# ga2 spread over 32 rows of the gate and up projections, with six places for its K-tiles

## The chip, the cores and the metric

The kernel runs on one NeuronCore of a Trainium2 chip. The metric is the device time of one execution in microseconds (us), as the median of several runs. The engines are TensorE (PE; its weight loads stand apart as PEld), VectorE (DVE), ScalarE (ACT), GpSimd (POOL) and SyncE (SP), whose queue issues nearly all loads here.

## What is computed

One layer of a diffusion backbone: a modulated RMS norm, an input projection to three parallel groups of heads (a recurrent scan, a short convolution, a Fourier mix), an output projection with a gated residual, then a modulated RMS norm, a SwiGLU FFN and a second gated residual. The six modulation vectors, 2048 long each, come from one product:

```python
m = jax.nn.silu(cvec) @ w + b
sh1, sc1, ga1, sh2, sc2, ga2 = jnp.split(m[:, None, :], 6, axis=-1)
...
x = x + ga1 * yx
x = x + ga2 * ffn(modulate(rms_norm(x, norm_ffn), sh2, sc2), w_gate, w_up, w_down)
```

The change concerns ga2 alone. It is not needed until the down projection's results are added to x. Token count is 256, D is 2048 and the FFN is 5632 wide.

## The kernel before

All numbers are float32. The large products keep full precision by splitting both sides into a high and a low part (the high part in a reduced matmul format), with three matmuls for one: high x high, high weight x low input, low weight x high input (`mm3`, line 249).

The FFN (`phase_ffn`, line 1101) has a gate/up part of 44 **rows** f, each giving 128 of the 5632 hidden columns, and a down part of 16 tiles. A row takes 4 **blocks** of weights: gate and up, each in two halves of 8 K-tiles. `wblock` (line 271) loads a block of 512 KB on SyncE's queue (w), ScalarE casts it to the high part (whi, line 266), and VectorE or, for every third block, POOL forms the low part (wlo, line 269). w, whi and wlo have three places each. TensorE then runs 24 matmuls for the block, so 96 for a row. At a row's end ScalarE takes silu of the gate half, VectorE multiplies it with the up half (line 1167, called vi in the code), and the product is split into HH (ScalarE) and HL (VectorE, line 269). Rows 0 and 1 are run together, while the normalised input XH and XL is formed.

w_mod's last four groups are formed on VectorE as a sum over K-tiles of a 128 x 512 piece of the matrix times one number per partition; 16 K-tiles make 512 of the 2048 x 4 columns, and 16 such vectors i = 0 to 15 make all four groups. Vectors 0 to 11 are formed earlier in the kernel. Vectors 12 to 15 are ga2 and are formed in the FFN by `modvec` (line 1081). Each K-tile is one load of 256 KB on SyncE's queue (line 1088) into one of two places of the buffer `ar`, and one multiply (line 1090, the first) or multiply-add (line 1092) on VectorE, into one of two accumulators. `modvec_end` (line 1094) sums over the partitions by four matmuls of a column of ones (line 233, out st), and adds the bias (line 1077).

`ar` lies in the memory of an earlier tile, so that the profile calls both the K-tiles and the accumulators XH; XH<-wmb is a K-tile's load. The profile's XH in gu<-XH is the normalised input, another tile of that name.

A scheduler orders each engine's instructions from the program text and its own estimate of times, after which each engine works through its list in order. `issue_after(vi.ins)` makes the VectorE instructions of the block under it stand behind row f's product in VectorE's list. The loads have no such tie and stand where the scheduler puts them. SyncE works through one list as well: a load that waits for its place holds all loads behind it.

Of the kernel before, what the change touches and what calls it, by code (L numbers as in the profile page):

```python
# [19 lines left out]
KT = D // P  # L20
# [180 lines left out]
class Builder:  # L201
# [876 lines left out]
                                     pm[:, :2 * npc].rearrange("p (j s) -> p j s", s=2)[:, :, s],  # L1078
                                     bm[:, 2 + g, o:o + npc], op=ALU.add)

    def modvec(self, i):

        nc, T = self.nc, self.t
        v2 = lambda ap: ap.rearrange("p (a t) -> p a t", t=L)
        acc = self.ar[:, 2 * (i % 2):2 * (i % 2) + 2]
        for k in range(KT):
            w = self.ar[:, 4 + 2 * (k % 2):6 + 2 * (k % 2)]
            nc.sync.dma_start(w, v2(self.a["wmb"][i, k]))
            if k == 0:
                nc.vector.tensor_scalar_mul(acc, w, self.sc[:, k, 1:2])  # L1090
            else:
                nc.vector.scalar_tensor_tensor(acc, w, self.sc[:, k, 1:2], acc, op0=ALU.mult, op1=ALU.add)  # L1092
# [8 lines left out]
    def phase_ffn(self, st):  # L1101
        tc, nc, a = self.tc, self.nc, self.a
        V, S, G, T = nc.vector, nc.scalar, nc.gpsimd, self.t
        fp = st.enter_context(tc.tile_pool(name="fp", bufs=2, reuse_waits="tile"))
        wsf = st.enter_context(tc.tile_pool(name="wsf", bufs=3, reuse_waits="tile"))
        fps = st.enter_context(tc.tile_pool(name="fps", bufs=2, space=PSUM, reuse_waits="tile"))
        X1 = self.X1
        XH = T(self.cp, [P, KT, L], F32R, "XH1")
        XL = T(self.cp, [P, KT, L], F32R, "XL1")
        self.modps, self.modtag = fps, "st"  # L1110

        T(fp, [P, 48], F32, "gap", 1)
        HH = T(fp, [P, NFF, L], F32R, "HH", 1)
        HL = T(fp, [P, NFF, L], F32R, "HL", 1)


        uh = self.uh
        ul = HL[:, NFF - 17:].rearrange("p f t -> p (f t)")[:, :KT * (L + 2)].rearrange("p (k t) -> p k t", k=KT)
        V.tensor_tensor(ul[:, :, L:], self.mod[:, 1].unsqueeze(2).to_broadcast([P, KT, 2]),
                        uh[:, :, L:].bitcast(F32), op=ALU.subtract)  # L1120
        for k in range(KT):
            V.scalar_tensor_tensor(ul[:, k, :L], X1[:, k], self.mod[:, 2, k:k + 1], uh[:, k, :L].bitcast(F32),  # L1122
                                   op0=ALU.mult, op1=ALU.subtract)
        self.heng = lambda n: nc.scalar
        self.cnt = 0
        self.leng = lambda n: nc.gpsimd if n <= 10 or n % 3 == 0 else nc.vector
        def gate_up(fs, xh, xl, norm=None):

            pgu = [T(fps, [P, 2 * L], F32, f"gu{w}")[:, :xh.shape[2]] for _ in fs for w in range(2)]
            for g in range(0, KT, G8):  # L1130
                for i, f in enumerate(fs):
                    for w in range(2):
                        with tc.issue_after(self.lasts):
                            h, lo = self.wblock(a["wgu"][f, w, :, g:g + G8], G8, G8, wsf)
                        for j in range(G8):
                            k = g + j
                            self.mm3(pgu[2 * i + w], h[:, j], lo[:, j], xh[:, k], xl[:, k], k == 0, k == KT - 1)
                        if norm is not None and (g, i, w) == (0, 0, 1):
                            S.copy(norm, self.rms_finish(self.x1s, fp, fps, L, "st", True))
            return pgu  # L1140

        for f in range(NFF):
            if f == 0:
                rs = T(fp, [P, L], F32, "rs", 1)
                pgs = gate_up((0, 1), uh, ul, rs)
                for k in range(KT):
                    xn = T(fp, [P, L], F32, "xn")
                    bias = self.mod[:, 1, k:k + 1]
                    V.scalar_tensor_tensor(xn, X1[:, k], self.mod[:, 2, k:k + 1], rs, op0=ALU.mult, op1=ALU.mult)  # L1149
                    S.activation(XH[:, k], xn, AF.Identity, bias=bias)  # L1150
                    V.scalar_tensor_tensor(XL[:, k], xn, bias, XH[:, k].bitcast(F32), op0=ALU.add, op1=ALU.subtract)  # L1151
                self.ar = self.wide(F32)[:, :, :L]
            sg = T(fp, [P, L], F32, "sg")
            if f < 2:
                pg, pu = pgs[2 * f:2 * f + 2]
                b = T(fp, [P, 2], F32, "b")
                V.tensor_copy(b[:, 0:1], pg[:, L:L + 1])
                V.tensor_copy(b[:, 1:2], pu[:, L:L + 1])
                V.tensor_tensor(sg, pg[:, :L], rs, op=ALU.mult)
                S.activation(sg, sg, AF.Silu, bias=b[:, 0:1])  # L1160
                su = T(fp, [P, L], F32, "xn")
                V.tensor_tensor(su, pu[:, :L], rs, op=ALU.mult)
                vi = V.scalar_tensor_tensor(sg, su, b[:, 1:2], sg, op0=ALU.add, op1=ALU.mult)
            else:
                pgu = gate_up((f,), XH, XL)
                S.activation(sg, pgu[0], AF.Silu)
                vi = V.tensor_tensor(sg, sg, pgu[1], op=ALU.mult)
            self.split(HH[:, f], HL[:, f], sg, S, V)
            if f % 8 == 3 and f < 32:
                with tc.issue_after(vi.ins):  # L1170
                    self.modvec(12 + f // 8)
            if f % 8 == 7 and f < 32:
                self.modvec_end(12 + f // 8)
        S.activation(self.x1s[:, :1], self.ones32[:, :1], AF.Sqrt)
        pst = T(fps, [P, L], F32, "st")
        for m in range(KT):
            pd = T(fps, [P, L], F32, "dn")
            for f0 in range(0, NFF, G8):
                nf = min(G8, NFF - f0)
                h, lo = self.wblock(a["wdn"][m, :, f0:f0 + nf], nf, G8, wsf)  # L1180
                for j in range(nf):
                    f = f0 + j
                    self.mm3(pd, h[:, j], lo[:, j], HH[:, f], HL[:, f], f == 0, f == NFF - 1)
            V.scalar_tensor_tensor(X1[:, m], pd, self.mod[:, 3, m:m + 1], X1[:, m], op0=ALU.mult, op1=ALU.add)
            sq = T(fp, [P, L], F32, "sq")
            S.square(sq, X1[:, m])
            self.rms_add(pst, sq, m)
            V.tensor_scalar_mul(X1[:, m], X1[:, m], self.vec("norm_final", m))
        rstd = self.rms_finish(pst, fp, fps, L, "st")
        rs = T(fp, [P, L], F32, "xn")  # L1190
        S.copy(rs, rstd)
        for k in range(0, KT, 2):
            o = self.ar[:, k:k + 2]
            for j in range(2):
                (G if k % 6 == 4 else V).tensor_tensor(o[:, j], X1[:, k + j], rs if k % 6 == 4 else rstd, op=ALU.mult)
            (nc.sync if k % 4 else nc.scalar).dma_start(self.out[:, k:k + 2], o)
# [16 lines left out]
```

## Time and profile before

| what | us |
|---|---|
| median of 3 runs | 1873.53 |
| lowest, highest | 1870.32, 1878.7 |
| the profiled execution | 1890.59 |
| its span, first to last instruction | 1888.8 |
| TensorE busy in it | 1733.7 |
| VectorE, ScalarE, POOL busy | 1107.4, 830.1, 802.8 |

The gate/up rows lie between 1080 and 1617 us of the span, the down tiles from 1617 to its end. The page has the busy shares; the chain of waits follows the work back from the last instruction, at each step to what released it, so its pieces add up to the span; a wait row names the engine that waited, what for, the total in us, the number of times and the longest one.

### The profile page before, as it was taken

How to read it: one execution, taken by the hardware profiler on the slowest of the kernel's cores; microseconds unless marked ns; L12 is line 12 of the kernel's file. 1: busy time of each engine (PE TensorE's matmuls, PEld its weight loads, DVE VectorE, ACT ScalarE, POOL GpSimd, SP SyncE). 2: the span in 40 equal slices, each digit the busy share in tenths (PEclk: the TensorE clock that was granted, in tenths of full speed). 3: DMA queues.
4: the chain of work that ended last, by engine and by line, in shares of the span. 5: the costliest groups of instructions: out<-in, count | busy, mean ns of one | idle time of the engine just before them, and what ended most of it. 6: DMA issues, size and time to landing. Idle time of an engine off the chain costs nothing.

```text
span 1888.8 us, 44826 instructions
## 1 busy us (share of the span) xinstructions
PE 1733.7 (92%) x18552; PEld 1587.2 (84%) x18552; DVE 1107.4 (59%) x1883; ACT 830.1 (44%) x1657; POOL 802.8 (43%) x718
## 2 busy tenths in 40 slices
PE   7888999999898899899898889999999999999997
PEld 4667898888787787687776688999999999999996
DVE  4445347787888777768784696454545434333223
ACT  2213355566655555444452443434344444433332
POOL 1223455467666665555661442322222232233332
PEclk9999999999999999999997989999999999999998
DMA  9884224355455443454441247676767666565554
GB/s 343 293 273 136 77 72 142 118 159 165 142 172 157 129 147 105 143 152 118 138 132 42 88 145 224 212 239 210 223 206 233 208 185 189 178 181 183 178 181 133
DMA packets 139229, 318.75 MB, mean 169 GB/s; under 512 B 14225, under 2 KB 40465, under 8 KB 139025
## 3 DMA queue, kind: packets, MB, share of 16 engines
q1 hardware_dynamic: 137936, 314.84, 53.1%
q8 instruction: 145, 2.38, 0.5%
q10 hardware_dynamic: 1088, 1.05, 0.2%
q14 instruction: 60, 0.48, 0.1%
HBM read 313.74 MB, written 2.10 MB: 167 GB/s over the span
## 4 chain that ended last, share of the span: by engine, by line
PE 40%; DVE 8%; DMA 6%; ACT 1%; issue 1%; POOL 0%; DVEq 0%; SPq 0%; ACTq 0%
PE gu L233 18%; PE dn L233 13%; DMA XH<-wmb 6%; PE pj L233 3%; PE acc L233 2%; PE st L233 1%; PE iv L233 1%; DVE XH L1092 1%; DVE macc L1063 1%; DVE XL L1151 1%; PE pp L233 1%; DVE HL L1122 0%; DVE xn L1149 0%; DVE XL L997 0%; DVE eb L729 0%
## 5 line engine op out<-in xcount | busy, mean ns | idle before, releaser
L269 POOL TENSOR_TENSOR wlo<-w,whi 128x512 fp32r<-128x512 f32 (+2 forms) x309 | 518.9, 1682 | 746.2 <-ACT whi L266 701.8
L266 ACT CAST whi<-w 128x1024 fp32r<-128x1024 f32 (+2 forms) x472 | 400.5, 849 | 565.7 <-PE gu L233 182.9
L233 PE MATMUL gu<-XH,wlo 128*128 128x256 f32 (+1 forms) x1408 | 398.5, 283 | 16.6 <-DVE wlo L269 14.9
L233 PE MATMUL gu<-XH,whi 128*128 128x256 f32 (+1 forms) x1408 | 397.8, 283 | 4.6 <-ACT whi L266 4.0
L269 DVE TENSOR_TENSOR wlo<-w,whi 128x1024 fp32r<-128x1024 f32 (+1 forms) x175 | 205.7, 1176 | 304.4 <-ACT whi L266 303.7
L233 PE MATMUL gu<-XL,whi 128*128 128x256 f32 x1344 | 376.6, 280 | 0.1
L233 PE MATMUL pj<-XH,whi 128*128 128x256 f32 x1016 | 285.6, 309 | 5.6 <-DVE XL L997 3.2
L233 PEld LDWEIGHTS gu<-XH,wlo 128*128 128x128 f32 x1408 | 269.0, 191 | 19.5 <-DVE wlo L269 17.2
L233 PEld LDWEIGHTS gu<-XH,whi 128*128 128x128 f32 x1408 | 271.3, 193 | 6.0 <-ACT whi L266 5.3
L233 PE MATMUL pj<-XL,whi 128*128 128x256 f32 x1016 | 257.6, 282 | 0.6 <-DVE XL L269 0.6
L233 PE MATMUL pj<-XH,wlo 128*128 128x256 f32 x1016 | 257.3, 282 | 0.0
L233 PEld LDWEIGHTS gu<-XL,whi 128*128 128x128 f32 x1344 | 255.2, 190 | 0.3 <-DVE XL L1151 0.3
L233 PE MATMUL dn<-HL,whi 128*128 128x256 f32 x704 | 199.4, 283 | 0.0
L233 PE MATMUL dn<-HH,whi 128*128 128x256 f32 x704 | 197.8, 281 | 0.0
L233 PE MATMUL dn<-HH,wlo 128*128 128x256 f32 x704 | 197.8, 281 | 0.0
L233 PEld LDWEIGHTS pj<-XH,whi 128*128 128x128 f32 x1016 | 181.8, 191 | 16.7 <-ACT whi L266 3.1
L233 PEld LDWEIGHTS pj<-XL,whi 128*128 128x128 f32 x1016 | 182.0, 191 | 2.4 <-issue 0.9
L233 PEld LDWEIGHTS pj<-XH,wlo 128*128 128x128 f32 x1016 | 181.0, 191 | 2.6 <-POOL whi L268 1.7
L1063 DVE SCALAR_TENSOR_TENSOR macc<-wm,sc,macc 128x512 f32<-128x512 f32 x180 | 170.1, 945 | 0.9
L233 PEld LDWEIGHTS dn<-HH,whi 128*128 128x128 f32 x704 | 135.1, 192 | 0.0
L233 PEld LDWEIGHTS dn<-HL,whi 128*128 128x128 f32 x704 | 132.1, 188 | 1.4
L233 PEld LDWEIGHTS dn<-HH,wlo 128*128 128x128 f32 x704 | 132.2, 188 | 0.0
(306 smaller groups left out, 2837.3 us busy)
## 6 DMA issues: line engine op xcount, KB each, us to landing
w<-wgu SPq DMA_DIRECT2D x176, 512.0 KB, 4.6
wm<-wmb SPq DMA_DIRECT2D x192, 256.0 KB, 3.1
w<-wdn SPq DMA_DIRECT2D x80, 512.0 KB, 4.3
w<-wib SPq DMA_DIRECT2D x148, 256.0 KB, 3.2
wm<-wma SPq DMA_DIRECT2D x64, 512.0 KB, 6.9
XH<-wmb SPq DMA_DIRECT2D x64, 256.0 KB, 4.1
w<-wout SPq DMA_DIRECT2D x48, 256.0 KB, 3.3
wa<-wia SPq DMA_DIRECT2D x16, 416.0 KB, 8.0
```

The lines of the kernel that those rows point to most:

```text
L233: self.last = self.nc.tensor.matmul(out, lhsT=lhsT, rhs=rhs, start=start, stop=stop)
L266: he.copy(hi, src)
L269: le.tensor_tensor(lo, src, hi.bitcast(F32), op=ALU.subtract)
L1063: V.scalar_tensor_tensor(acc, w, self.sc[:, k, 1:2], acc, op0=ALU.mult, op1=ALU.add)
L1092: nc.vector.scalar_tensor_tensor(acc, w, self.sc[:, k, 1:2], acc, op0=ALU.mult, op1=ALU.add)
L1151: V.scalar_tensor_tensor(XL[:, k], xn, bias, XH[:, k].bitcast(F32), op0=ALU.add, op1=ALU.subtract)
```

## The change

Two K-tiles of ga2 stand in each of the rows 0 to 31, instead of 16 in each of the rows 3, 11, 19 and 27. They use six places of `ar` by the K-tile's number, instead of two. A vector's column matmuls and its bias stand in the text after row 8, 16, 24 and 32, instead of 7, 15, 23 and 31.

```diff
-    def modvec(self, i):
+    def modvec(self, i, ks):
...
-        for k in range(KT):
-            w = self.ar[:, 4 + 2 * (k % 2):6 + 2 * (k % 2)]
+        for k in ks:
+            w = self.ar[:, 4 + 2 * (k % 6):6 + 2 * (k % 6)]
             nc.sync.dma_start(w, v2(self.a["wmb"][i, k]))
...
-            if f % 8 == 3 and f < 32:
+
+            if f < 32:
                 with tc.issue_after(vi.ins):
-                    self.modvec(12 + f // 8)
-            if f % 8 == 7 and f < 32:
-                self.modvec_end(12 + f // 8)
+                    self.modvec(12 + f // 8, (2 * (f % 8), 2 * (f % 8) + 1))
+            if f % 8 == 0 and 0 < f <= 32:
+                self.modvec_end(11 + f // 8)
```

SyncE's list before, at the second burst (row 11's text). w_ numbers are weight blocks in the order of the rows, XH<-wmb is a K-tile of ga2:

```order
L276 DMA w_2854_17681<-wgu 128x1024
L276 DMA w_2860_17718<-wgu 128x1024
L1088 DMA XH_2684_16225<-wmb 128x2x256 x2
L276 DMA w_2863_17748<-wgu 128x1024
L1088 DMA XH_2684_16225<-wmb 128x2x256
L276 DMA w_2866_17778<-wgu 128x1024
L1088 DMA XH_2684_16225<-wmb 128x2x256
L276 DMA w_2869_17808<-wgu 128x1024
L1088 DMA XH_2684_16225<-wmb 128x2x256 x2
L276 DMA w_2875_17845<-wgu 128x1024
```

The same place of SyncE's list now. The numbers of blocks are the same up to the second, longer one:

```order
L276 DMA w_2845_17575<-wgu 128x1024
L1088 DMA XH_2684_16225<-wmb 128x2x256
L276 DMA w_2848_17605<-wgu 128x1024
L1088 DMA XH_2684_16225<-wmb 128x2x256
L276 DMA w_2851_17635<-wgu 128x1024
L276 DMA w_2854_17665<-wgu 128x1024
L276 DMA w_2860_17706<-wgu 128x1024
L1088 DMA XH_2684_16225<-wmb 128x2x256 x2
L276 DMA w_2863_17736<-wgu 128x1024
L276 DMA w_2866_17766<-wgu 128x1024
L276 DMA w_2869_17796<-wgu 128x1024
L276 DMA w_2875_17837<-wgu 128x1024
```

Before, sixteen K-tiles of one vector alternate with the weights of three rows, and none stand in the five rows after. Now two stand among the four weight loads of each row. In a pattern that repeats every three rows they stand once as a pair, right ahead of w_2863, whose place is freed by a low part on POOL; in the two other rows they stand singly ahead of blocks of VectorE.

VectorE's list before, from row 11's product (sg<-sg,gu on line 1167) on:

```order
L1167 TENSOR_TENSOR sg_17429<-sg_17429,gu_2829_17431 128x256
L1090 TENSOR_SCALAR XH_2684_16225<-XH_2684_16225,sc_121 128x2x256
L1092 SCALAR_TENSOR_TENSOR XH_2684_16225<-XH_2684_16225,sc_121 128x2x256
L269 TENSOR_TENSOR HL_15885<-sg_17429,HH_15884 128x256
L1092 SCALAR_TENSOR_TENSOR XH_2684_16225<-XH_2684_16225,sc_121 128x2x256
L269 TENSOR_TENSOR wlo_17683<-w_2854_17681,whi_17682 128x1024
L1092 SCALAR_TENSOR_TENSOR XH_2684_16225<-XH_2684_16225,sc_121 128x2x256
L269 TENSOR_TENSOR wlo_17720<-w_2860_17718,whi_17719 128x1024
L1092 SCALAR_TENSOR_TENSOR XH_2684_16225<-XH_2684_16225,sc_121 128x2x256 x2
```

And now, from the same product:

```order
L1167 TENSOR_TENSOR sg_17441<-sg_17441,gu_2829_17443 128x256
L1092 SCALAR_TENSOR_TENSOR XH_2684_16225<-XH_2684_16225,sc_121 128x2x256 x2
L269 TENSOR_TENSOR HL_15885<-sg_17441,HH_15884 128x256
L269 TENSOR_TENSOR wlo_17667<-w_2854_17665,whi_17666 128x1024
L269 TENSOR_TENSOR wlo_17708<-w_2860_17706,whi_17707 128x1024
L1167 TENSOR_TENSOR sg_17572<-sg_17572,gu_2844_17574 128x256
L1092 SCALAR_TENSOR_TENSOR XH_2684_16225<-XH_2684_16225,sc_121 128x2x256
L269 TENSOR_TENSOR wlo_17768<-w_2866_17766,whi_17767 128x1024
L1092 SCALAR_TENSOR_TENSOR XH_2684_16225<-XH_2684_16225,sc_121 128x2x256
L269 TENSOR_TENSOR HL_15885<-sg_17572,HH_15884 128x256
```

Multiply-adds stood between the low parts of all blocks of some three rows; now two stand behind each row's product, either together or with one low part between them.

The first place changes most: SyncE's list had two K-tiles ahead of the block w_2709 (row 3's first), and has six there now.

```order
L276 DMA w_2700_16311<-wgu 128x1024
L276 DMA w_2703_16341<-wgu 128x1024
L1088 DMA XH_2684_16225<-wmb 128x2x256 x2
L276 DMA w_2709_16378<-wgu 128x1024
L276 DMA w_2712_16408<-wgu 128x1024
L276 DMA w_2715_16438<-wgu 128x1024
L276 DMA w_2718_16468<-wgu 128x1024
```

The same place now:

```order
L276 DMA w_2703_16349<-wgu 128x1024
L1088 DMA XH_2684_16225<-wmb 128x2x256 x6
L276 DMA w_2709_16390<-wgu 128x1024
L276 DMA w_2712_16420<-wgu 128x1024
L276 DMA w_2715_16450<-wgu 128x1024
L1088 DMA XH_2684_16225<-wmb 128x2x256 x3
L276 DMA w_2718_16480<-wgu 128x1024
```

The six are the K-tiles of rows 0 to 2; the three behind them are let go by the multiplies of rows 0 and 1.

The column matmuls of the first vector stood in TensorE's list a quarter into row 7 and at row 8's start; they stand three quarters into row 8 and at row 9's start now, and so with the other vectors.

## Rows read from the trace of the kernel before

**Rows 1.** The page, part 1: busy us (share of the span) xinstructions.
```profile
PE 1733.7 (92%) x18552; PEld 1587.2 (84%) x18552; DVE 1107.4 (59%) x1883; ACT 830.1 (44%) x1657; POOL 802.8 (43%) x718
```
**Rows 2.** The chain of waits from 1126 to 1485 us, by line.
```profile
by line: PE gu L233 54.7%; DMA XH<-wmb 30.1%; DVE XH L1092 6.8%; issue 2.2%; DMA w<-wgu 1.4%; DVE wlo L269 1.4%; PE st L233 0.9%; POOL wlo L269 0.7%; ACT whi L266 0.6%; DVE sg L1167 0.5%; DVE XH L1090 0.4%; DVEq L1092 0.1%; DVE XL L1151 0.1
```
**Rows 3.** Row 3's product; then the chain's long pieces: start us, us, what.
```profile
1144.35 0.42 DVE L1167 TENSOR_TENSOR sg<-sg,gu 128x256 f32<-128x256 f32 x1 [3.49 <-PE gu L233]
...
1195.75 43.67 PE gu L233 x384
...
1290.17 43.66 PE gu L233 x384
...
1389.55 43.66 PE gu L233 x384
...
1481.62 135.79 PE gu L233 x1152
```
**Rows 4.** The timeline of SyncE's queue in the second burst: start us, us, instruction.
```profile
1248.80 0.34 SPq L276 DMA_DIRECT2D w<-wgu  x1
1252.16 1.49 SPq L1088 DMA_DIRECT2D XH<-wmb  x2
1253.75 0.85 SPq L276 DMA_DIRECT2D w<-wgu  x1
```
**Rows 5.** Waits of SyncE's queue, 1126 to 1482 us: total, times, longest.
```profile
SPq L1088 <- DVE XH L1092: 36.5, 43, 2.5
...
SPq L1088 <- DMA XH<-wmb: 29.7, 25, 2.7
```
**Rows 6.** Waits of TensorE, 1144 to 1482 us.
```profile
PE gu L233 <- DVE wlo L269: 14.1, 9, 3.1
PE st L233 <- DVE XH L1092: 3.6, 2, 2.7
```
**Rows 7.** The K-tiles' loads: ns to issue (min/median/max); KB each, us to landing.
```profile
L1088 SPq DMA_DIRECT2D XH<-wmb x64: 539/540/1343, 1115.5 to 1467.0; - x64
...
XH<-wmb SPq DMA_DIRECT2D x64, 256.0 KB, 4.1
```
**Rows 8.** TensorE's timeline at the end of the fourth vector.
```profile
1480.90 0.72 PE L233 MATMUL st<-consts,XH 128*128 128x2 f32 x6
```
**Rows 9.** Windows of the third burst: us, busy by engine, PEclk, DMA share, GB/s.
```profile
1350.00:1358.00 8.00, 5.41 (x42) 5.21 (x41) 4.01 (x6) 2.10 (x2) 1.15 (x1) 0.93 0.59 214
...
1374.00:1382.00 8.00, 5.80 (x37) 5.83 (x38) 4.44 (x5) 3.70 (x5) 1.62 (x2) 0.79 0.73 220
```
**Rows 10.** SyncE's timeline at the first K-tiles.
```profile
1115.47 1.46 SPq L1088 DMA_DIRECT2D XH<-wmb  x2
```
**Rows 11.** A POOL block; a cast; landings at 1482-1617 and 1334-1376 us; the page's GB/s.
```profile
1216.02 2.40 POOL L269 TENSOR_TENSOR wlo<-w,whi 128x1024 fp32r<-128x1024 f32 x1 [5.76 <-ACT whi L266]
...
1504.26 1.05 ACT L266 CAST whi<-w 128x1024 fp32r<-128x1024 f32 x1 [1.45 <-PE gu L233]
...
w<-wgu SPq DMA_DIRECT2D x43, 512.0 KB, 4.5
...
w<-wgu SPq DMA_DIRECT2D x10, 512.0 KB, 5.9
...
GB/s 343 293 273 136 77 72 142 118 159 165 142 172 157 129 147 105 143 152 118 138 132 42 88 145 224 212 239 210 223 206 233 208 185 189 178 181 183 178 181 133
```
**Rows 12.** VectorE: multiply-adds (ns, min/median/max), their waits, then its timeline.
```profile
L1092 DVE SCALAR_TENSOR_TENSOR XH<-XH,sc x60: 744/753/2798, 1145.2 to 1471.8; 128x512 f32<-128x512 f32 x60
...
  DMA XH<-wmb: 58.6, 44
...
1208.12 2.42 DVE L269 TENSOR_TENSOR HL<-sg,HH 128x256 fp32r<-128x256 f32 x1 [0.83 <-ACT HH L266]
...
1218.65 1.23 DVE L269 TENSOR_TENSOR wlo<-w,whi 128x1024 fp32r<-128x1024 f32 x1 [0.48 <-ACT whi L266]
1219.80 0.42 DVE L269 TENSOR_TENSOR HL<-sg,HH 128x256 fp32r<-128x256 f32 x1
```

## Prediction

> **What bounds the kernel now.** I read the page first, then the chain of waits through the gate/up rows of the FFN, the PE waits there, and SyncE's timeline. TensorE is busy for 92% of the span [rows 1], so the time is TensorE's work plus the holes in it, and the question is which holes this change can close. In the chain over 1126 to 1485 us, 30.1% is a load of w_mod (XH<-wmb) and 54.7% are gate/up matmuls [rows 2]: in that stretch loads of the modulation matrix end many waits, though TensorE needs nothing from them but a few column matmuls.
>
> The long pieces of the chain show where the time lies [rows 3]. Between the four bursts of loads TensorE runs four rows, 384 matmuls, in 43.66 us without a break: 10.92 a row, 114 ns a matmul. The four rows with a burst are what lies between: from the end of row 3 (the product on line 1167 at 1144.35) to 1195.75 are 51.40 us; from 1195.75 + 43.67 = 1239.42 to 1290.17, 50.75; from 1333.83 to 1389.55, 55.72; from 1433.21 to 1481.62, 48.41. Together 206.3 us for 16 rows that would take 174.7 unbroken: 31.6 us too much.
>
> The mechanism stands in SyncE's timeline [rows 4]: a weight load goes out at 1248.80, then the queue stands until 1252.16, when two wmb loads go, and only at 1253.75 the next weight load. A wmb load waits for its place, that is for the multiply-add that reads the place, and that one for the landing of the load before it. With two places, 16 K-tiles make a ladder of landings, and the weights queue behind it. From 1126 to 1482 us SyncE waits 36.5 + 29.7 us on this ladder [rows 5]. TensorE feels it as late weights: 14.1 us for VectorE's wlo, and 3.6 us of column matmuls that wait for the last multiply-add [rows 6].
>
> **The change, part by part.** *Work.* The same 64 loads of 256 KB, 60 multiply-adds, 4 first multiplies and 4 sets of column matmuls remain. Nothing is saved in work; all is in waits.
>
> *The ladder goes.* A load now needs the multiply-add six K-tiles back, three rows earlier (four K-tiles across a vector's end, since 16 is no multiple of 6, so two rows). It lands in 4.1 us in the median [rows 7] and is used some 20 us later, so VectorE should not wait for one. Of the 31.6 us I leave what stays: the eight column matmuls of a vector, six of which took 0.72 us [rows 8], 0.96 for eight and 3.8 for four vectors. Removable: 27.8 us. The lower bound is what TensorE is shown waiting, 14.1 + 3.6 = 17.7. The higher value is the nearer one, since holes also drop the granted clock: 0.93 and 0.79 in two windows of 8 us of the third burst [rows 9], (0.07 + 0.21) x 8 = 2.2 us by these two alone.
>
> *The start pays.* At the first place six wmb loads stand ahead of a weight load instead of two. Two took SyncE 1.46 us [rows 10], so four more cost up to 2.9. Where they land, VectorE's normalisation holds TensorE's next inputs anyway. Bounds 0 and 2.9; I take 1.5, the middle, as the rows show no way to place it better.
>
> *POOL's slot.* w, whi and wlo have three places each and every third wlo is POOL's, so POOL's blocks always share a slot. Its cycle is landing 4.5 + cast 1.05 + wlo 2.40 = 7.95 us; POOL's blocks come every 5.76 + 2.40 = 8.16 us [rows 11]: 0.21 us of room. In every third row two wmb loads now stand just ahead of a weight load of that slot (w_2863 in the order shown). They take 2 x 0.54 us to issue [rows 7], and their 0.52 MB 1.5 us at 343 GB/s, the highest slice of the page [rows 11]: 2.6 us. In nine such rows 23, less the room of 28 rows x 4/3 = 37.3 cycles, 7.8: at most some 15. The least is 0, since TensorE comes to a block two blocks of 24 matmuls, 5.46 us, after its cast begins, and 5.46 - 1.05 - 2.40 leaves 2.0 us. I take 3, near the low end: the median landing is 4.5 us outside the bursts and 5.9 in the worst burst alone [rows 11].
>
> *VectorE's row end.* Two multiply-adds of 0.75 us [rows 12] now stand behind a row's product, ahead of the next wlo or the one after. VectorE's wlo has 5.46 - 1.05 - 1.23 = 3.2 us of room, which covers 1.5 us; without that cover each microsecond would be TensorE's. I take 0. But a multiply-add took 2.80 us at worst, and HL 2.42 instead of 0.42 while POOL worked [rows 12]: a collision costs some 2.05 us. Product 0.42, HL 0.42, two multiply-adds 1.50 and one collision make 4.39, over the room by 1.2: the upper end is 28 x 1.2 = 34 us, the lower 0. The row nearest to the case is the unbroken stretch at 1208, where a blocked HL made no hole.
>
> The Trainium skill speaks against the change here: "SBUF — State Buffer", section "Who interferes with whom", says that a VectorE instruction with two SBUF inputs and a GpSimd instruction that reads SBUF shut each other out for a whole instruction. The durations of 2.42 and 2.80 us agree with it; if by that rule each of the 28 rows collided, those 34 us would come back and the sum would be a loss.
>
> *Column matmuls* move most of a row behind the last multiply-add, so their 3.6 us of waiting goes (counted above).
>
> Sum: 27.8 - 1.5 - 3.0 = **23.3 us**. The profiled execution took 1890.59 us, so 1867.3 on its own scale; it lies 17.1 us above the median of the three runs. On the median, 1873.53 - 23.3 = **1850 us**.
>
> *A pace that I can't forecast.* Rows without any hole took 10.92 us up to row 31 and 135.79 / 12 = 11.32 from row 32 on [rows 3]: 4 ns a matmul. What sets it, the rows don't say; the change moves holes and column matmuls, and may move it too. All 28 rows at the slower pace cost 11 us; the last 12 at the faster one give 5. I take neither and put both into the range.
>
> **Rivals.**
> 1. *Holes close, but the pace turns slow* (gain 9.4 to 18). For it: nothing says that rows 4 to 31 keep the faster one. 23.3 - 11 = 12: about 1861. In the same band: SyncE still stands a little because each wmb load waits for a multiply-add behind a row's product. By the order the weight load behind it waits for a wlo that is later still, so I count a few tenths of a us a row.
> 2. *Collisions at every row end.* 34 us back: 1873.5 - 27.8 + 34 = about 1880; in every third row, 11 back, about 1861. Against it: the unbroken stretches carry a blocked HL without a hole.
> 3. *Slower: POOL's slot sets the pace of all rows.* If weights land as in the third burst, 5.9 us, the cycle is 9.35 instead of 8.16: 37.3 x 1.19 = 44 us, 1873.5 - 27.8 + 44 = about 1890. It decides from a landing of 8.16 + 27.8/37.3 - 3.45 = 5.5 us on. For it: 2.6 MB a row in 10.92 us are 240 GB/s, in all rows instead of in bursts. Against it: only one load in three counts, and mostly no wmb load stands right ahead of it.
>
> **How the numbers follow.** Likeliest (gain 18 to 33: holes gone, costs small) 0.70; rival 1, 0.17; rival 2, 0.08; rival 3, 0.05. A measurement here tells about 0.5%, 9.4 us, from no change. Faster by more are the first two, 0.87; same 0.08; slower 0.05. The range goes from 1839 (27.8 plus the faster pace at the end, no cost at start or slot, and 2 us of rounding in the terms) to 1864 (23.3 less 11 of pace and a little more); not quite 2 in 10 lie outside, most of it above.
>
> **What would show it.** Right: no share of XH<-wmb worth naming in the chain; VectorE's wait for wmb (58.6 us now [rows 12]) near 0; rows 4 to 31 at 10.9 to 11.3 us each, with no hole over 1 us. The start is wrong if row 3 ends more than 3 us later than at 1144.35. The slot term is wrong if TensorE waits for POOL's wlo by more than 6 us in all; rival 2 holds if it waits for VectorE's in most rows; rival 3 if POOL's blocks come every 9 us. The forecast is wrong if the chain still shows holes of microseconds in these rows, or if time is lost after row 32, which the change doesn't touch.

## The result and the profile after

| | before | after |
|---|---|---|
| median of 10 runs, us | 1881.69 | 1862.76 |
| lowest, highest | 1870.32, 1897.35 | 1852.99, 1875.63 |
| the profiled execution | 1890.59 | 1853.2 |
| its span | 1888.8 | 1851.4 |

The ratio is 0.990, with a 95% interval from 0.9869 to 0.9931: 18.9 us faster, between 13 and 25. The ten runs of before have a median 8 us above that of the three shown ahead of the prediction. A later comparison of the same pair, in experiment e8_change_again, gave 0.9899 (0.9833 to 0.9965). A ratio leaves out runs more than 1.5% above the fastest of their kernel, which in the comparison of e1, e2 and e3 are 7 of the 17 of before, so those three state the gain rather too low.

The two profiled executions differ by 37.4 us of span, about twice as much as the medians. So the first thing to settle is how much of that is the change. The page and the chain of the changed kernel, the chain in the same window as [rows 2]:

```profile
PE 1715.0 (93%) x18552; PEld 1570.0 (85%) x18552; DVE 1113.0 (60%) x1883; ACT 829.9 (45%) x1657; POOL 801.3 (43%) x718
```
```profile
by line: PE gu L233 75.2%; DMA w<-wgu 12.4%; POOL wlo L269 6.8%; ACT whi L266 3.0%; DVE xn L1149 0.7%; DVE XH L1092 0.7%; PE st L233 0.6%; issue 0.5%; DVE wlo L269 0.3%; ACT XH L1150 0.1%; DVE XL L1151 0.1%; ACTq L266 0.1%; ACT sg L1166 0.1
```

The load of w_mod, 30.1% of the chain before, is gone from it; gate/up matmuls have gone from 54.7% to 75.2%. The instruction counts on TensorE are the same. Now the long pieces of the chain, to set beside [rows 3]:

```profile
1200.97 87.18 PE gu L233 x768
1288.14 0.79 PE st L233 x8
1288.93 65.02 PE gu L233 x551
...
1416.93 49.25 PE gu L233 x432
...
1469.55 119.81 PE gu L233 x1056
```

Where four bursts cut the rows before, TensorE now runs eight rows in a piece of 87.18 us and, behind a set of column matmuls, 551 matmuls more. The last piece covers rows 33 to 43. It also shows something else: 119.81 / 1056 = 113.5 ns a matmul, where before rows 32 to 43 took 135.79 / 1152 = 117.9 [rows 3]. The change touches nothing there. A second execution of before (e10_before_again) was profiled for this, and a second of the change (e8_change_again). Row ends are the products on line 1167, as in the first row of [rows 3]; times in us:

| execution | span | up to the first gate/up matmul | from there to row 3's product | row 3's to row 31's | to row 43's | down projection to its last matmul |
|---|---|---|---|---|---|---|
| before | 1888.8 | 1080.3 | 64.1 | 336.8 | 136.3 | 255.1 |
| before again | 1879.5 | 1087.8 | 64.1 | 334.3 | 131.3 | 245.9 |
| change | 1851.4 | 1081.5 | 63.4 | 312.9 | 131.6 | 245.9 |
| change again | 1861.4 | 1091.7 | 63.9 | 312.1 | 131.6 | 246.0 |

The products of rows 3 and 31, from VectorE's timeline (start us, us, instruction): the changed kernel, then before again.

```profile
1144.95 0.42 DVE L1167 TENSOR_TENSOR sg<-sg,gu 128x256 f32<-128x256 f32 x1 [2.85 <-PE gu L233]
...
1457.89 0.42 DVE L1167 TENSOR_TENSOR sg<-sg,gu 128x256 f32<-128x256 f32 x1 [0.59 <-PE gu L233]
```
```profile
1151.88 0.42 DVE L1167 TENSOR_TENSOR sg<-sg,gu 128x256 f32<-128x256 f32 x1 [3.48 <-PE gu L233]
...
1486.19 0.42 DVE L1167 TENSOR_TENSOR sg<-sg,gu 128x256 f32<-128x256 f32 x1 [0.58 <-PE gu L233]
```

Read by columns, the table is plain. **Rows 4 to 31** take 21 to 25 us less with the change, in either pair. The last two columns don't tell the kernels apart: before again has the changed kernel's numbers there. So of the 37.4 us of the first pair, 23.9 are the change and 13.9 are a pace of TensorE that differs between executions, less half a microsecond that the parts ahead took back. The time up to the first gate/up matmul, which the change does not touch either, differs by 11 us among the four. These two are of the size by which runs of one kernel lie apart, 23 to 27 us; that they make up most of it is not shown.

The waits say the same. Of the changed kernel, SyncE's queue, 1126 to 1471 us (to set beside [rows 5]), and TensorE, 1144 to 1471 us (beside [rows 6]):

```profile
SPq L276 <- POOL wlo L269: 113.7, 39, 3.6
SPq L276 <- DVE wlo L269: 76.3, 64, 2.4
...
SPq L1088 <- DVE XH L1092: 19.0, 33, 2.5
```
```profile
PE gu L233 <- POOL wlo L269: 1.5, 2, 1.1
PE gu L233 <- ACT whi L266: 0.2, 1, 0.2
```

The ladder's second half, the wait of a K-tile's load for the load before it (29.7 us, 25 times), no longer occurs; a K-tile's load still waits 19.0 us for places, but little hangs on that: SyncE's weight loads wait longer for a wlo (113.7 and 76.3 us, the first two rows), and TensorE's 17.7 us of waits are 1.7. In the second execution of the change they are 0.4. XH<-wmb has no share in the chain of either.

### The profile page after: what moved, and what is told of

Its sections match the earlier page's. It is cut to its first block, busy times and chain, and to the rows that moved or that the text cites. A ratio compares the mean times of both kernels' runs of the same rounds, so it can differ in the third digit from the quotient of the medians.

```text
span 1851.4 us, 44772 instructions
## 1 busy us (share of the span) xinstructions
PE 1715.0 (93%) x18552; PEld 1570.0 (85%) x18552; DVE 1113.0 (60%) x1883; ACT 829.9 (45%) x1657; POOL 801.3 (43%) x718
## 4 chain that ended last, share of the span: by engine, by line
PE 45%; DVE 8%; DMA 2%; ACT 2%; POOL 1%; issue 1%; DVEq 0%; ACTq 0%
PE gu L233 21%; PE dn L233 13%; PE pj L233 4%; DMA w<-wgu 2%; PE acc L233 2%; PE iv L233 2%; PE st L233 2%; POOL wlo L269 1%; PE pp L233 1%; DVE macc L1063 1%; DVE XL L1151 1%; ACT whi L266 1%; DVE HL L1122 0%; DVE eb L729 0%; DVE xn L1149 0%
## 5 line engine op out<-in xcount | busy, mean ns | idle before, releaser
L233 PE MATMUL gu<-XH,whi 128*128 128x256 f32 (+1 forms) x1408 | 393.7, 280 | 4.2 <-ACT whi L266 3.7
L233 PE MATMUL gu<-XH,wlo 128*128 128x256 f32 (+1 forms) x1408 | 392.1, 280 | 3.6 <-POOL wlo L269 2.8
L233 PE MATMUL gu<-XL,whi 128*128 128x256 f32 x1344 | 372.5, 277 | 0.1
L233 PEld LDWEIGHTS gu<-XH,whi 128*128 128x128 f32 x1408 | 267.0, 190 | 5.9 <-ACT whi L266 5.2
```

The source lines that it names most:

```text
L233: self.last = self.nc.tensor.matmul(out, lhsT=lhsT, rhs=rhs, start=start, stop=stop)
```

## The experiments

Two theories stood against each other at first. **Ladder**: K-tiles in a burst stop the weights behind them in SyncE's queue; what counts is that they no longer stand in bursts. **Places or bytes**: two places are too few wherever the K-tiles stand, or the burst's 4 MB take the weights' bandwidth.

**e1_spread_two_places.** The change, with two places:

```diff
-            w = self.ar[:, 4 + 2 * (k % 6):6 + 2 * (k % 6)]
+            w = self.ar[:, 4 + 2 * (k % 2):6 + 2 * (k % 2)]
```

> Two K-tiles a row as in the change, but with the two places of before. Theory (the burst is the fault: with one use a row, a load has a whole row of 10.9 us for a landing of 4 to 5 us, so two places are enough): as fast as the change, 15 to 25 us below the kernel before, and XH<-wmb under 3% of the chain in rows 4 to 31. Rival (the places are the fault: a load waits for the multiply-add just behind a row's product, holds SyncE's queue there and the weights behind it): under half of the gain, 0 to 10 us, with SyncE's waits for the multiply-adds above 30 us.

Measured: 1860.34 us, ratio 0.9893 (0.9828 to 0.9959). Rows 4 to 31 take 313.1 us, XH<-wmb is gone from their chain, and SyncE waits 15.4 us there for multiply-adds, half of what the rival asked. TensorE has one wait, 1153 to 1467 us:

```profile
PE gu L233 <- POOL wlo L269: 0.2, 1, 0.2
```

Spreading alone gives all of it, as far as these runs can tell; no use of the four added places shows.

**e2_bursts_six_places.** The reverse: before, with six places (`k % 2` made `k % 6` in the same line).

> Sixteen K-tiles in each of the four bursts as before, with the six places of the change. Theory (the burst is the fault): the ladder of landings goes, but four loads of 256 KB now stand between two weight loads, and 4 MB come on top of the weights within two or three rows, so holes of 3 to 6 us a burst stay: 5 to 15 us below the kernel before. Rival (the places are the fault): 18 to 28 us below it, as the change.

Measured: 1870.67 us, ratio 0.9955 (0.9923 to 0.9988), 8.4 us. Rows 4 to 31 take 319.2 us in its profile, so there it has some 15 to 18 of the 21 to 25. By the timings it has half, and its median lies 10.3 us above e1's in the same comparison. SyncE's waits, 1126 to 1486 us, and the chain's pieces in the first burst:

```profile
SPq L1088 <- DVE XH L1092: 21.8, 34, 2.6
...
SPq L1088 <- DMA XH<-wmb: 1.0, 1, 1.0
```
```profile
1162.00 6.86 DMA XH<-wmb
1177.93 60.41 PE gu L233 x528
```

The ladder of landings is gone with the places (29.7 us to 1.0), but a burst is still in the way: one K-tile's load is 6.86 us of the chain here. Either edit breaks the ladder; the 6.1 us by which rows 4 to 31 are longer than e1's are what the bursts still cost, since the two executions run the same share of matmuls, 41%, at the slower of TensorE's two paces.

**e9_bursts_eighth_of_bytes.** Before, but each K-tile's load brings 64 of 512 columns, 32 KB instead of 256. The places are cleared once at the start.

```diff
-            nc.sync.dma_start(w, v2(self.a["wmb"][i, k]))
+            nc.sync.dma_start(w[:, :1, :64], v2(self.a["wmb"][i, k])[:, :1, :64])
...
+                G.memset(self.ar[:, 4:8], 0.0)
```

> The kernel before, bursts and two places, but each K-tile's load brings only 64 of 512 columns, 32 KB instead of 256: the rest of ga2 is left out (the places are cleared once). It parts the two things a burst does, to hold SyncE's queue on landings and to take bandwidth from the weights. Theory (the ladder of landings holds the queue): a landing shortens from 4.1 us to some 2.5, but the ladder stays, so a good half of the holes stays: rows 3 to 31 take 320 to 332 us against 336.8, 5 to 15 us below the kernel before. Rival (bandwidth: 4 MB a burst beside the weights): holes under 4 us, rows 3 to 31 take 309 to 315 us, 18 to 28 below.

Measured: 1880.05 us, ratio 0.9981 (0.9932 to 1.003). Seven eighths of the burst's bytes are gone, and rows 4 to 31 still take 339.8 us. Its queue's waits and loads (KB each, median us to landing), 1126 to 1486 us, and TensorE's waits:

```profile
SPq L1088 <- DVE XH L1092: 36.0, 44, 2.6
SPq L1088 <- DMA XH<-wmb: 25.7, 24, 2.7
```
```profile
w<-wgu SPq DMA_DIRECT2D x118, 512.0 KB, 4.4
XH<-wmb SPq DMA_DIRECT2D x62, 32.0 KB, 3.1
```
```profile
PE gu L233 <- DVE wlo L269: 16.4, 8, 3.1
```

The ladder has nearly the same waits as [rows 5], and TensorE waits 16.4 us where it waited 14.1 [rows 6]. A load of an eighth of the bytes lands in 3.1 us instead of 4.0 to 4.2, so most of a landing is not its bytes. The theory had expected 2.5, and 320 to 332 us for the rows. The share of time in which the DMA engines were busy with the queue's packets fell too, from 69.0% to 59.7% in this window, from before to e9. So the burst cost what it did by the order of the queue. A share of bandwidth as its cause falls.

**e3_first_tile_only.** The change, with only the first K-tile of each vector, so 15 of 16 loads and multiply-adds of ga2 are left out (the column matmuls stay):

```diff
-        for k in ks:
+        for k in ks[:1] if ks[0] == 0 else ():
```

> The change without 15 of the 16 K-tiles of each vector of ga2: the sum is left out, its first tile and the column matmuls stay. It is the floor of what the gate/up rows cost without the loads. If the terms of the prediction are right (start 1.5 us, POOL's slot 3 us, VectorE 0), it is 2 to 8 us faster than the change, 21 to 31 below the kernel before. If POOL's slot or VectorE's collisions eat a good part of what the change could give, it is 10 to 25 us faster than the change.

Measured: 1850.32 us, ratio 0.9847 (0.9794 to 0.99). Rows 4 to 31 take 308.9 us, 4.0 less than with the change and 27.9 less than before: what the K-tiles still cost is at most about 4 us of the 28 they cost in bursts. Half of the 4 is the pace: 6% of e3's matmuls in these rows run at the slower one, 23% of the change's, and 455 matmuls at 4.4 ns are 2.0 us. By the medians it lies 10 us below the change, by a ratio whose interval overlaps the change's; taken alone that would speak for the rival (10 to 25), not the theory (2 to 8), but the profile's number is the better one, since it leaves out the part ahead and the pace of the end.

**e5_no_pool** and **e11_two_places_no_pool.** What is left is POOL's slot, if the prediction's term is right: the chain of the changed kernel goes through it at rows 4 to 7.

```profile
1144.92 2.41 POOL wlo L269
1147.35 4.11 DMA w<-wgu
1151.56 1.06 ACT whi L266
1152.69 2.40 POOL wlo L269
1155.11 4.50 DMA w<-wgu
1159.70 1.06 ACT whi L266
1160.84 2.40 POOL wlo L269
```

From one POOL block to the next are 7.77 and 8.15 us, which is the landing, the cast and the low part, one behind the other. e5 is the change and e11 is e1, both with the low parts from the eleventh block on, those of the down projection too, on VectorE alone:

```diff
-        self.leng = lambda n: nc.gpsimd if n <= 10 or n % 3 == 0 else nc.vector
+        self.leng = lambda n: nc.gpsimd if n <= 10 else nc.vector
```

> The change with all low parts of the gate/up and down weights from the eleventh block on formed by VectorE, none by POOL. Theory (POOL's slot, whose cycle of about 8.0 us barely fits, makes the holes that the change leaves): the holes of rows 4 to 31 over 0.25 us fall from 2.4 us to under 1, and rows 3 to 31 take 2 to 4 us less at the same pace. Rival (they come from VectorE standing behind a row's product, or from two multiply-adds there): with a third more work on VectorE holes grow to 5 us or more and rows 3 to 31 take longer than the change's 312.9.

> Two places, two K-tiles a row, and no low part on POOL after the tenth block. Both took holes away alone (0.6 and 0.0 us left). If they add, no hole over 0.25 us in rows 4 to 31 and 20 to 30 us below the kernel before; with the pace left to chance it can't be told from the run with two places alone by more than 5 us.

Measured: 1866.01 us, 0.9884 (0.9828 to 0.994), and 1866.12 us, 0.9886 (0.9824 to 0.9947). TensorE waits for nothing in rows 4 to 31 of either, so the holes do go; but rows 4 to 31 take 317.1 us in both, 4 more than with POOL. The chain of e5 says why:

```profile
1206.52 90.56 PE gu L233 x768
1297.08 0.79 PE st L233 x8
1297.86 90.56 PE gu L233 x768
```

That is 117.9 ns a matmul, without a hole and without an end, where the change ran 768 in 87.18 us. The slot is worth the change's holes, 0.7 to 2.4 us in its two executions, and the slower pace ate them: 82% of the matmuls run at it. How that came about is not shown, but one thing differs from the change: in e5 and e11 all four sets of column matmuls run whole, as in the chain above (four columns, eight instructions), where with the change only one of four does. The last section counts what followed whole sets. On the time the experiment says nothing.

**e4_columns_each_row.** To see what sets the pace: the change, with a set of four needless column matmuls in the text behind each of the rows 33 to 43.

```diff
+            if f > 32:
+                pm = T(fps, [P, 2 * L], F32, "st")
+                for j in range(4):
+                    self.mm(pm[:, 2 * j:2 * j + 2], X1[:, j, :P], self.cst("one"), True, True)
```

> The change with four needless column matmuls behind each of the rows 33 to 43, on data that lie there. It asks what sets TensorE's pace, 10.88 or 11.31 us a row without a hole. If column matmuls can set it, the rows from 33 to 43 don't all run at one pace: both show, and the pace changes only at such matmuls. If the pace belongs to a stretch of time (the clock, the load of the chip), the eleven rows keep the pace that row 32 had, plus some 0.5 to 1 us a row for the added matmuls.

Measured: 1864.08 us, one execution. Rows 34 to 43 take 12.0 to 12.4 us each, of which 0.79 are the column matmuls. The chain has both paces:

```profile
1478.16 11.41 PE gu L233 x96
...
1499.31 2.62 PE gu L233 x22
```

Behind a whole set 96 matmuls take 11.41 us, 118.9 ns each with the start of the piece. The 22 matmuls behind a set that was broken off after its first column take 2.62 us, where the same 22 took 2.70 us at 1463.11, 3.6 ns a matmul more. It looked as if sets brought the slower pace and single column matmuls the faster one.

**e6_one_column** and **e7_two_places_one_column** tested that: one column matmul in the text of row 36, which the scheduler puts into row 34, added to the change and to e1.

```diff
+            if f == 36:
+                pm = T(fps, [P, 2 * L], F32, "st")
+                self.mm(pm[:, :2], X1[:, 0, :P], self.cst("one"), True, True)
```

> The change with one needless column matmul in row 34. Theory (a column matmul among the others sets TensorE's pace, and a single one sets the faster pace in most cases, as 14 of 16 single ones did in the run with the first K-tile only): rows 35 to 43 take 10.9 us and the down tiles 15.4 in the profile, and the median is 2 to 8 us below the change's. Rival (the pace of a stretch is chance, or belongs to the chip's state): no difference in the median, 0.2 us more work.

> Two places and two K-tiles a row, with the one needless column matmul of row 34. If both earlier findings hold (two places are enough, one column matmul sets the faster pace), the fastest version so far: 22 to 32 us below the kernel before, 2 to 10 below the change. If the pace is chance, as the run with two places: 15 to 25 below the kernel before.

Measured: e6 1867.71 us, 0.9887 (0.9821 to 0.9953); e7 1859.25 us, 0.9858 (0.9803 to 0.9914). The added matmul did opposite things. The chain of e6, then that of e7:

```profile
1480.95 13.96 PE gu L233 x122
1494.90 0.12 PE st L233 x2
1495.02 110.11 PE gu L233 x934
```
```profile
1474.35 14.48 PE gu L233 x122
1488.83 0.12 PE st L233 x2
1488.94 105.98 PE gu L233 x934
```

In e6 a pace of 13.96 / 122 = 114.4 ns became 110.11 / 934 = 117.9. In e7 it went from 14.48 / 122 = 118.7 to 113.5. So the theory that a single column matmul always brings the faster pace fell; that it mostly does is not refuted. e7 has the lowest median of the complete versions, 1859.25 us; its interval and those of e1 and the change overlap, so none of the three is shown to be better.

**e8_change_again** and **e10_before_again** are the two kernels themselves, as controls; their profiles stand in the table above.

> The change again, beside the three below on the same chip. All theories: 13 to 25 us below the kernel before. If TensorE's pace is set at random in each execution, the down tiles come either at 15.4 or at 16.0 us, and its runs spread over some 20 us as in the first comparison.

> The kernel before once more, for a second profile of it. If the bursts' holes are of the program and not of that one execution, rows 3 to 31 take 330 to 342 us again with 18 to 26 us of holes over 0.25 us, while the time up to the first gate/up matmul and the pace of the down tiles may differ.

Measured: 1868.56 us, ratio 0.9899 (0.9833 to 0.9965), and 1881.31 us in one execution. The holes of e10 over 0.25 us come to 17.1 us, a little under the 18 to 26 expected; counted the same way, the first execution of before has 21.0.

## Why the prediction held, point by point

**What the ladder cost: right, if a little high.** The prediction took 27.8 us as removable from rows 4 to 31. With nearly all K-tiles away (e3) they are 27.9 us shorter than in the profiled execution of before, and 25.4 shorter than in the second, whose holes are smaller; 1 to 3 us of either are e3's faster pace. So the agreement with 27.9 is partly luck. The lower bound, 17.7 us of TensorE's own waits, would have been too low, since the waits leave out starts that are only a little late: 63 matmuls of before start 125 to 250 ns after the one ahead, which adds 6.0 us; with the change 9 do, which adds 0.9. That the price came from the stop in the queue is shown by e9 (the bytes cut to an eighth, no gain) and by e1 and e2 (either cure breaks the ladder).

**The start: too high, harmlessly.** 1.5 us were charged for six loads ahead of row 3's weights. From the first gate/up matmul to row 3's product it takes 63.4 and 63.9 us instead of 64.1 in both executions of before: no cost.

**POOL's slot: right in place, charged a little high.** 3 us were charged. The slot is the chain in rows 4 to 7 and again from 1379 to 1417 us, and the change's holes are 2.4 us over the rows (those over 0.25 us between two matmuls, added up over the trace) and 0.7 in its second execution, with 1.5 us as wait rows for POOL's wlo, under the 6 us that would have refuted the term. Without POOL's blocks they are 0.

**VectorE's row end: right that it costs nothing.** The multiply-adds and the low part of the product in VectorE's groups of the changed kernel, 1144 to 1471 us (count | busy us, mean ns | idle before), then of before, 1144 to 1482 us:

```profile
L1092 DVE SCALAR_TENSOR_TENSOR XH<-XH,sc 128x512 f32<-128x512 f32 x55 | 54.1, 983 | 0.3
L269 DVE TENSOR_TENSOR HL<-sg,HH 128x256 fp32r<-128x256 f32 x30 | 33.3, 1109 | 2.9 <-ACT HH L266 2.7
```
```profile
L1092 DVE SCALAR_TENSOR_TENSOR XH<-XH,sc 128x512 f32<-128x512 f32 x60 | 55.7, 929 | 59.0 <-DMA XH<-wmb 58.6
L269 DVE TENSOR_TENSOR HL<-sg,HH 128x256 fp32r<-128x256 f32 x28 | 23.7, 847 | 4.8 <-ACT HH L266 4.8
```

VectorE's idle time before its multiply-adds, nearly all of it a wait for K-tiles, fell from 59.0 us to 0.3, as the prediction asked, though a K-tile landed in 5.0 us in the median and not in 4.1. Collisions with POOL did not go away: HL took 1109 ns in the mean instead of 847, where it needs 420 alone. That the multiply-adds brought them is not shown: HL takes 1061 ns in e3, which has none in these rows. Against those 420, and 748 for a multiply-add, 20.7 and 12.9 us of VectorE's time went in them. The long ones end 0.3 to 0.6 us behind the end of one of POOL's low parts. This agrees with what the Trainium skill says in "SBUF — State Buffer", section "Who interferes with whom", of VectorE and GpSimd shutting each other out. But TensorE has no wait row for VectorE in these rows, so the room of 3.2 us at a block was enough. Rival 2 fell. (Its two prices have different bases: about 1880 leaves out the 4.5 us of start and slot, and about 1861 counts them.) Rival 3 fell too: POOL's blocks come every 8.3 us in the mean over the rows, 8 of 37 more than 9 us behind the one before, and not every 9.

**The sign of rows and holes: met in the mean.** Rows 4 to 31 take 312.9 / 28 = 11.2 us, inside 10.9 to 11.3, but from product to product they take 9.7 to 12.8, and one hole is 1.07 us, over the 1 us that the sign allowed.

**The sum.** Rows 4 to 31 gave 23.9 us in the first pair (24.6 with the start), beside 23.3 forecast, and 21 to 25 over all pairs of profiles. By the medians it is 18.9, with 23.3 inside the interval of 13 to 25. The median came out at 1862.76 instead of 1850.2, 1.2 us under the range's upper end. Of these 12.6 us 8.2 are the base: the forecast was subtracted from a median of three runs, 1873.53, which ten runs put at 1881.69. The other 4.4 are the gain, 18.9 against 23.3. The 18.9 lie just inside the likeliest band of 18 to 33, and the interval reaches into rival 1's. So the time alone would not tell the two apart; the rows do.

**The pace: rightly left open.** Rival 1 feared the slower pace in all rows. Of the 2688 matmuls of rows 4 to 31, 615 run at it (116 to 125 ns from start to start) in the changed kernel's profile, 819 in its second, 1093 in e1 and 2205 in e5, but 465 and 773 in the two of before. It moved single executions by more than the prediction charged for start and slot together, 4.5 us.

## What to carry to other kernels

Work that nothing waits for can still be dear in an engine's or queue's list: a load that waits for its place stops every load behind it, so read what stands behind a waiting instruction, and place filler loads one or two at a time rather than in bursts; fewer bytes would not have helped here. Cost such an edit between two product rows of the same stretch, not by two spans: here the spans differed by 37.4 us, and the change was worth 21 to 25 in the rows and 18.9 by the medians. And profile the old kernel twice before giving the change a difference in a part that it does not touch.

## What the runs showed of the hardware

TensorE has two paces for the same unbroken stream of matmuls, at a granted clock of 1.00 (the upper level, 2.4 GHz) in both. Windows of e6 ahead of and behind its added column matmul (us, busy by engine with counts, PEclk, DMA share, GB/s):

```profile
1400.00:1470.00 70.00, 70.00 (x620) 70.00 (x619) 39.34 (x43) 31.01 (x39) 21.17 (x9) 1.00 0.72 223
1500.00:1600.00 100.00, 100.00 (x851) 100.00 (x850) 42.47 (x42) 42.57 (x54) 27.57 (x12) 1.00 0.62 186
```

70.00 / 620 is 112.9 ns and 100.00 / 851 is 117.5, TensorE busy throughout in both. A stream keeps its pace for 100 us and more (the 934 matmuls of e6 and of e7). From row 3 on, all changes of pace found in these profiles but one stand at a matmul of another shape or a late start, and a small one is enough: in e7 a single start 201 ns behind the one ahead, at 1419.9 us, parts 113 from 118. The one that stands at neither: in the second execution of the change the down projection turns slower at 1722 us with no two starts over 123 ns apart. The down projection shows it too; before, then before again, one of its tiles each:

```profile
1637.56 15.74 PE dn L233 x132
```
```profile
1636.74 15.17 PE dn L233 x132
```

The pace was worth 9.2 us in the down projection and 4.7 to 5.0 in rows 32 to 43. What picks it was not found: a single column matmul was followed by the slower pace in e6 and by the faster one in e7. But the cases lean. Over the gate/up rows of all 13 profiles, a whole set of four column matmuls was followed by the slower pace in 21 of 22 cases (8 of them in e4, 8 in e5 and e11), and one column by itself by the faster in 41 of 54 (14 of 16 in e3). This is a count of what came after, no cause shown, and the two executions of before differ from row 32 on in one and the same program. A way to force the faster pace would be worth more, in an execution that runs at the slower one, than what the change left.
